# Closing the tile context ahead of the wait for the last stores in a Winograd convolution

## The chip, the core and the metric

The kernel runs on one core of one Trainium2 chip. The metric is the time of one execution on the device in microseconds (us); smaller is better. The core's engines run their own instruction streams and meet only through semaphores (counters): TensorE (PE in the profile, its weight loads PEld), VectorE (DVE), ScalarE (ACT), GpSimd (POOL) and SyncE (SP), which computes nothing and issues transfers. A name with a q behind it (SPq, POOLq) stands for that engine's sequencer.

## The reference

```python
def setup_inputs():
    batch, c_in, h, w, c_out = 16, 64, 64, 64, 128
    return {
        "x": np.random.randn(batch, c_in, h, w).astype(np.float32),
        "weight": np.random.randn(c_out, c_in, 3, 3).astype(np.float32) * 0.1,
    }

def reference(x, weight):
    x_pad = np.pad(x, ((0, 0), (0, 0), (1, 1), (1, 1)), mode='constant')
    output = np.zeros((batch, c_out, h, w), dtype=np.float32)
    ...
    output[b, co] += weight[co, ci, kh, kw] * x_pad[b, ci, kh:kh+h, kw:kw+w]
```

It is a 3x3 convolution with padding 1: 16 images of 64 channels and 64 x 64 points, 128 output channels. The input has 16.8 MB, the output 33.6 MB.

## The kernel before

**The work.** Two images are loaded as one pair, 128 partitions (two images times 64 channels) by 64 rows by 64 columns. There are 8 pairs, and each is worked off in 4 blocks of 8 row pairs. Over the rows the kernel uses a transformation that makes two output rows out of fewer products: GpSimd (for the first block VectorE) adds neighbouring rows to `ss`, ScalarE casts the rows to 16 bits in `xs`, TensorE multiplies in a loop of 8 rounds, one for each pair (L294 is the only matmul line of the loop), ScalarE copies two accumulators to `ut` (L204), and VectorE adds `ut` to the other accumulators and writes the output rows to a buffer called a home (L234).

**The transfers.** `load` is called by SyncE and by GpSimd; `store` (its transfer is on L109) by SyncE for the first image of a pair and by ScalarE for the second. The last pair's images go out in two pieces each, rows 0 to 32 and 32 to 64. A home that a later output uses again is guarded by a semaphore of its own (`s_out`). Every store whose home is used by nobody later counts on the one semaphore `s_end`, 16 for each store; `n_end` is the number of these stores.

**The order.** All of this stands in one critical section (L73, `tc.tile_critical`), in which the program itself sets every wait; each engine has its stream written out. When an engine has reached the end of the section it drains, and GpSimd waits for the drains of the others. Behind the section stand these two lines (L305 and L306):

```python
    tc.no_sync_barrier()
    SP.wait_ge(s_end, SP.to_reg(16 * n_end)).then_inc(s_done, 1)
```

The wait's threshold is moved to a register first. After it the function returns, the context `tc` is left (`with _tile.TileContext(nc) as tc:`, L332), and leaving it emits the closing instructions, which carry L332 in the profile: a few waits and a drain on SyncE; a crossing of all engines, in which each drains and reports and GpSimd gathers the reports and releases all; a drain and a clear of the context's semaphores on GpSimd (EVENT_SEMAPHORE_RANGE_CLEAR); and a second such crossing. The semaphores that are cleared there are those that were taken by `tc.alloc_semaphore`, through the helper `sem`, and a few of the context's own. L321 carries the instructions ahead of the program.

Of the kernel before, what the change touches and what calls it, by code (L numbers as in the profile page):

```python
# [25 lines left out]
def kernel(tc: tile.TileContext, x: bass.AP, weight: bass.AP, out: bass.AP):  # L26
    nc = tc.nc
# [3 lines left out]
    def sem(name):  # L31
        return tc.alloc_semaphore(name)
# [8 lines left out]
    s_act = sem("s_act")  # L41
    s_dve = sem("s_dve")
    s_out = {}
    s_end, s_done = sem("s_end"), sem("s_done")

    c_sum, c_cast, c_bank = sem("c_sum"), sem("c_cast"), sem("c_bank")

# [11 lines left out]
    PE, ACT, DVE, POOL, SP = nc.tensor, nc.scalar, nc.vector, nc.gpsimd, nc.sync  # L59
# [13 lines left out]
    with tc.tile_critical(sync_engine=EngineType.Pool):  # L73
# [51 lines left out]
        pieces, n_end = {}, 0  # L125
# [176 lines left out]
                                    mm.then_inc(s_pe, 1)  # L302
                            i += 1

    tc.no_sync_barrier()  # L305
    SP.wait_ge(s_end, SP.to_reg(16 * n_end)).then_inc(s_done, 1)  # L306


# [28 lines left out]
```

## Time and profile before

| | us |
|---|---|
| median of 3 runs | 126.46 |
| lowest and highest | 126.23, 126.65 |
| the profiled execution | 125.64 |
| its span, from the first to the last instruction of the program | 123.8 |

| engine | busy us | share of the span |
|---|---|---|
| TensorE (matmul) | 108.0 | 87% |
| VectorE | 84.1 | 68% |
| ScalarE | 67.2 | 54% |
| GpSimd | 38.9 | 31% |

The profile is of one execution. Its 1.84 us beside the span lie ahead of the first and behind the last instruction of the program and are not in the trace. Times inside the trace count from the first instruction. A row of the trace that names an engine, a line and an operation has its count, then minimum, median and maximum in ns, then the start of the first and of the last in us. A semaphore instruction's row shows when it fired and for how long it ran; the time that it waited before is in the list of waits. The page's slices cut the span in 40 equal parts of 3.1 us.

### The profile page before, as it was taken

The page shows a single profiled execution, that of the slowest core. Times are in us where ns is not written, and L with a number is a line of the kernel's source. Part 1 is how long each engine was busy: PE and PEld are TensorE (multiplying, and loading weights), DVE is VectorE, ACT ScalarE, POOL GpSimd, SP SyncE. Part 2 cuts the span into 40 slices and gives each one's busy share as a digit, 9 for nine tenths or more (in the row PEclk, how much of TensorE's full clock was granted, in tenths as well). Part 3 has the DMA queues.
Part 4 walks back from the last instruction along what each step waited for, and adds up shares of the span by engine and source line. Part 5 has one row for each costly group of instructions (what it writes and reads, how often), then busy time and mean ns, then how long its engine had stood idle before and what let it go on. Part 6 is the DMA issues. An engine that isn't in the chain of part 4 may idle for free.

```text
span 123.8 us, 2533 instructions
## 1 busy us (share of the span) xinstructions
PE 108.0 (87%) x989; PEld 56.7 (46%) x989; DVE 84.1 (68%) x133; ACT 67.2 (54%) x100; POOL 38.9 (31%) x30
## 2 busy tenths in 40 slices
PE   5969999999999999999999999999999999970000
PEld 1525555555555555555555555555555555530000
DVE  0067777877787778777877787788888887771000
ACT  4266656666666666666666566656665666520000
POOL 2207457170708270615054423233241103000000
PEclk9999999999999999999999999999999999999555
DMA  4999999999999999999999999999999999999993
GB/s 108 392 442 424 365 320 326 387 296 363 365 352 344 381 396 379 392 380 389 387 392 377 388 387 381 380 395 413 383 400 412 422 383 429 432 426 416 429 426 156
DMA packets 4467, 46.46 MB, mean 375 GB/s; under 512 B 496, under 2 KB 624, under 8 KB 1264
## 3 DMA queue, kind: packets, MB, share of 16 engines
q1 hardware_dynamic: 2160, 25.46, 50.0%
q10 hardware_dynamic: 1296, 16.78, 31.7%
q0 software_dynamic: 1008, 4.19, 16.6%
q14 instruction: 3, 0.02, 0.0%
HBM read 17.07 MB, written 33.55 MB: 409 GB/s over the span
## 4 chain that ended last, share of the span: by engine, by line
PE 82%; DVE 2%; DVEq 0%; issue 0%
PE bank L294 82%; DVE home L234 2%; DVEq L73 0%
## 5 line engine op out<-in xcount | busy, mean ns | idle before, releaser
L234 DVE TENSOR_TENSOR home<-bank,ut 128x512 f32<-128x512 f32 x128 | 81.9, 686 | 21.9 <-PE bank L294 21.7
L294 PE MATMUL bank<-xs,Wt 64*128 64x504 f16 (+3 forms) x768 | 87.5, 373 | 0.0
L294 PEld LDWEIGHTS bank<-xs,Wt 64*128 64x128 f16 x768 | 43.6, 94 | 38.6
L204 ACT COPY ut<-bank 128x512 f32<-128x512 f32 x64 | 34.4, 589 | 37.7 <-PE bank L294 37.7
L115 POOL TENSOR_TENSOR ss<-pair 128x1024 f16<-128x1024 f16 (+1 forms) x9 | 17.1, 1906 | 39.1 <-PE bank L294 32.4
L294 PE MATMUL bank<-ss,Wt 64*128 64x504 f16 (+1 forms) x192 | 26.5, 377 | 1.1 <-PEq L273 1.1
L115 POOL TENSOR_TENSOR ss<-home 128x1024 f16<-128x1024 f32 x7 | 16.5, 2364 | 14.5 <-PE bank L294 12.5
L121 ACT CAST xs<-home 128x1024 f16<-128x1024 f32 (+2 forms) x16 | 16.9, 1057 | 0.3 <-DMA home<-in_x_dram 0.3
L121 ACT COPY xs<-pair 128x1024 f16<-128x1024 f16 (+2 forms) x16 | 16.9, 1059 | 0.0
L294 PEld LDWEIGHTS bank<-ss,Wt 64*128 64x128 f16 x192 | 10.8, 94 | 10.8 <-issue 1.5
L95 POOL DMA_DIRECT2D pair<-in_x_dram x7 | 4.0, 577 | 8.6 <-DMA home<-in_x_dram 8.6
L248 PE MATMUL bank<-zeros 128*128 128x512 f16 x11 | 4.2, 540 | 1.4 <-DVE zeros L219 1.4
L220 DVE TENSOR_TENSOR Wt<-Wt 128x384 f16<-128x384 f16 x1 | 0.4, 358 | 4.8 <-ACT Wt L197 4.8
L197 ACT CAST Wt<-bank 128x384 f16<-128x384 f32 x3 | 1.2, 487 | 3.1 <-PE bank L257 3.1
L248 PEld LDWEIGHTS bank<-zeros 128*128 128x128 f16 x11 | 1.2, 124 | 3.1 <-DVE zeros L219 1.4
L197 ACT ACT_TABLE_LOAD x1 | 1.3, 1283 | 0.9 <-PEq L321 0.9
L257 PEld LDWEIGHTS bank<-ident,w 128*64 128x64 f16 x18 | 1.1, 209 | 1.0 <-POOL w L173 1.0
L173 POOL CAST w<-w_raw 128x576 f16<-128x576 f32 x1 | 0.7, 662 | 2.4 <-DMA w_raw<-in_weight_dram 2.4
L257 PE MATMUL bank<-ident,w 128*64 128x128 f16 x18 | 1.3, 299 | 0.1
L115 DVE TENSOR_TENSOR ss<-home 128x512 f16<-128x512 f32 x2 | 1.3, 688 | 0.0
L219 DVE MEMSET zeros<- 128x256 uint32 x1 | 0.3, 272 | 1.1 <-PEq L321 1.1
L221 DVE TENSOR_TENSOR Wt<-Wt 128x384 f16<-128x384 f16 x1 | 0.4, 359 | 0.0
(6 smaller groups left out, 0.9 us busy)
## 6 DMA issues: line engine op xcount, KB each, us to landing
out_dram<-home SPq DMA_DIRECT2D x7, 2048.0 KB, 23.0
out_dram<-home ACTq DMA_DIRECT2D x7, 2048.0 KB, 18.2
home<-in_x_dram SPq DMA_DIRECT2D x3, 2048.0 KB, 21.2
home<-in_x_dram SPq DMA_DIRECT2D x2, 1024.0 KB, 6.5
pair<-in_x_dram POOLq DMA_DIRECT2D x2, 1024.0 KB, 16.8
out_dram<-home SPq DMA_DIRECT2D x2, 1024.0 KB, 11.6
out_dram<-home ACTq DMA_DIRECT2D x2, 1024.0 KB, 11.1
pair<-in_x_dram POOLq DMA_DIRECT2D x3, 512.0 KB, 29.3
```

The source lines that it names most:

```text
L95: eng.dma_start(pairs[p][:, lo:hi, :], x_rows[128 * p : 128 * p + 128, lo:hi, :]).then_inc(s_in[p][k], 16)
L115: return eng.tensor_add(ss[:, lo : lo + n, :], v[:, lo : lo + n, 0, :], v[:, lo : lo + n, 1, :])
L121: return ACT.copy(xs[:, lo:hi, :], pairs[m // NB][:, lo:hi, :])
L173: when(POOL.tensor_copy(w16, w_raw), s_w, 16).then_inc(s_pool, 1)
L197: ACT.copy(wrow(g), flat[wp_bank[g]][:, 0 : 3 * CO]), s_pe, i + 1
L204: ACT.copy(uts[n % 2][b2], banks[(6 * n + b2) % 8]), s_pe, tiles(n, 1 + b2)
L220: when(DVE.tensor_sub(wrow(G21), wrow(G2), wrow(G1)), s_act, 2)
L221: when(DVE.tensor_sub(wrow(G01), wrow(G0), wrow(G1)), s_act, 3)
L234: DVE.tensor_add(rows(homes[OUT_HOME[p][b2]])[:, j0 : j0 + RB, i, :], banks[(6 * n + 2 + 2 * i + b2) % 8], uts[n % 2][b2],),
L248: PE.matmul(flat[7], zeros[:, 0:128], zeros)
L257: mm = PE.matmul(flat[wp_bank[g]][q : q + 64, k * CO : k * CO + CO], w16[:, t::9], ident)
L294: mm = PE.matmul(acc[b2][:, lo - j0 : hi - j0, c_lo:c_hi], Wt[p0 : p0 + 64, wi, kw, :], rhs, start=i == 0, stop=i == n - 1,)
```

## The change

The context is ended inside the function (`tc.close()`, which ends the trace of the body and goes to its end block) and compiled there (`tc.compile()`, which emits the closing instructions). SyncE's wait for the last stores is traced after that, with a constant instead of a register, and no longer increments `s_done`, which is gone. `s_end` is taken from `nc` instead of the context, so that the context's clear leaves it out; behind the wait SyncE clears it with an instruction of its own, and its number is given back, which emits nothing. When the `with` block is left, the context is compiled already.

```diff
     s_out = {}
-    s_end, s_done = sem("s_end"), sem("s_done")
+
+    s_end = nc.alloc_semaphore("s_end")
...
-    tc.no_sync_barrier()
-    SP.wait_ge(s_end, SP.to_reg(16 * n_end)).then_inc(s_done, 1)
+
+
+    tc.close()
+    tc.compile()
+    SP.wait_ge(s_end, 16 * n_end)
+    SP.sem_clear(s_end)
+    nc.release_semaphore(s_end)
```

## The prediction

> **What bounds the kernel now.** I read the page first, then the chain of work that ended last, then the end of the span piece by piece. The page's head, the two DMA lines of its slices and its HBM line:
>
> ```profile
> span 123.8 us, 2533 instructions
> ...
> DMA  4999999999999999999999999999999999999993
> GB/s 108 392 442 424 365 320 326 387 296 363 365 352 344 381 396 379 392 380 389 387 392 377 388 387 381 380 395 413 383 400 412 422 383 429 432 426 416 429 426 156
> ...
> HBM read 17.07 MB, written 33.55 MB: 409 GB/s over the span
> ```
>
> From the second slice to the last but one the 16 DMA engines are busy for 90% or more. So the transfers fill the span, and the last slice (3 tenths, 156 GB/s) is the only stretch at the end where they do not. The chain that ended last does not show this, because it is followed through engines and not through the stores:
>
> ```profile
> 7.92 101.44 PE bank L294 x948
> 109.36 1.90 DVE home L234 x3
> 111.26 0.60 DVEq L73
> ```
>
> It stops at 111.9 us, when the engines have nothing left to compute. What holds the remaining 11.9 us is seen in the timeline (start, duration) and in SyncE's own waits:
>
> ```profile
> 111.28 0.33 SPq L109 DMA_DIRECT2D out_dram<-home  x1
> 111.89 0.34 ACTq L109 DMA_DIRECT2D out_dram<-home  x1
> ```
>
> ```profile
> SPq L306 <- DMA out_dram<-home: 10.7, 1, 10.7
> SPq L332 <- PEq L332: 0.7, 2, 0.6
> ```
>
> L109 is the line of `store`: the last two stores are issued at 111.28 and 111.89. L306 is SyncE's wait for `s_end`, once, for 10.7 us. L332 is the line that opens the context: what its end emits carries that line. The stretches from there on, with DMA share and GB/s as the last two columns:
>
> ```profile
> core 0: us, PE busy (x) PEld busy (x) DVE busy (x) ACT busy (x) POOL busy (x), PEclk, DMA share, GB/s
> 111.90:112.90 1.00, 0.00 (x0) 0.00 (x0) 0.00 (x0) 0.00 (x0) 0.00 (x0) 1.00 0.82 344
> 112.90:114.00 1.10, 0.00 (x0) 0.00 (x0) 0.00 (x0) 0.00 (x0) 0.00 (x0) 1.00 1.00 425
> 114.00:116.00 2.00, 0.00 (x0) 0.00 (x0) 0.00 (x0) 0.00 (x0) 0.00 (x0) 0.58 1.00 426
> 116.00:118.00 2.00, 0.00 (x0) 0.00 (x0) 0.00 (x0) 0.00 (x0) 0.00 (x0) 0.50 1.03 434
> 118.00:120.00 2.00, 0.00 (x0) 0.00 (x0) 0.00 (x0) 0.00 (x0) 0.00 (x0) 0.50 0.98 418
> 120.00:122.00 2.00, 0.00 (x0) 0.00 (x0) 0.00 (x0) 0.00 (x0) 0.00 (x0) 0.50 0.92 389
> 122.00:122.30 0.30, 0.00 (x0) 0.00 (x0) 0.00 (x0) 0.00 (x0) 0.00 (x0) 0.50 0.01 0
> 122.30:123.80 1.50, 0.00 (x0) 0.00 (x0) 0.00 (x0) 0.00 (x0) 0.00 (x0) 0.50 0.00 0
> ```
>
> For ten microseconds only the stores run. They stop just after 122.0. Then come 1.5 us in which neither an engine nor a transfer does anything: this is where the change works.
>
> **The change part by part.** First the end as it stands, from the sequencer rows of lines 73 (the end of the critical section), 306 and 332 (count, min/median/max ns, first and last start):
>
> ```profile
> L73 SPq DRAIN  x1: 123/123/123, 111.7 to 111.7; - x1
> L73 ACTq DRAIN  x1: 153/153/153, 112.3 to 112.3; - x1
> L73 POOLq NOP  x1: 13/13/13, 112.5 to 112.5; - x1
> ```
>
> ```profile
> L306 SPq MOVE  x1: 40/40/40, 111.9 to 111.9; - x1
> L306 SPq EVENT_SEMAPHORE  x1: 17/17/17, 122.6 to 122.6; - x1
> ```
>
> ```profile
> L332 POOLq DRAIN  x1: 41/41/41, 112.5 to 112.5; - x1
> ...
> L332 SPq EVENT_SEMAPHORE  x1: 28/28/28, 122.7 to 122.7; - x1
> ...
> L332 SPq DRAIN  x2: 7/7/7, 122.9 to 122.9; - x2
> L332 POOLq EVENT_SEMAPHORE  x2: 17/17/17, 123.0 to 123.0; - x2
> ...
> L332 POOLq DRAIN  x1: 119/119/119, 123.1 to 123.1; - x1
> ...
> L332 PEldq EVENT_SEMAPHORE  x2: 51/51/51, 123.1 to 123.7; - x2
> ...
> L332 POOLq EVENT_SEMAPHORE  x2: 17/17/17, 123.6 to 123.7; - x2
> ...
> L332 POOLq EVENT_SEMAPHORE_RANGE_CLEAR  x1: 225/225/225, 123.3 to 123.3; - x1
> L332 SPq EVENT_SEMAPHORE  x1: 17/17/17, 123.7 to 123.7; - x1
> ```
>
> Read in order: SyncE's wait on `s_end` fires at 122.6. SyncE then passes its own context waits (122.7) and drains (122.9). GpSimd, already drained at 112.5, gathers the five engines and releases them (123.0), which the others see at 123.1. It drains again for 119 ns, clears the kernel's counters in 225 ns, gathers a second time and releases at 123.7. The last instruction is TensorE's receipt, 51 ns from 123.7. Nothing in this chain needs the stores. It stands behind them only because SyncE is the late one of the five.
>
> *Moved: the closing chain.* With the context closed ahead of SyncE's wait, the chain is started by whoever is last to leave the section: GpSimd's NOP at 112.5, as ScalarE drains at 112.3. It took 123.8 - 122.6 = 1.2 us, so it ends near 113.7. No DMA is in it, and it is moved past no issue: both last stores are issued by 112.2. Its cover is the stores in flight to 122.0 and the 10.7 us wait. Some 9 us of cover are left over. Without that cover, with the last store landing less than 1.2 us after its issue, it would cost the 1.2 us as now. As `s_end` stands among the ids to be cleared but is kept out, the clear may come as two; a second 225 ns lies under the same cover.
>
> *Removed:* the MOVE of 40 ns at 111.9, which went with the constant, and the increment of `s_done`. Both are worth nothing: the stores cover the first, and the wait's own 17 ns carry the second.
>
> *Added behind the wait:* one clear on SyncE. Behind it on SyncE nothing is queued, and nobody waits for it. It costs the pitch between two SyncE instructions, 0.1 us (122.6 to 122.7), and its own duration. No row shows a clear on SyncE. From below stands SyncE's 17 ns semaphore instruction; from above the same operation on GpSimd, 225 ns, for the counters of the whole kernel (29 are declared in it). One counter instead of those, and SyncE's drain at 7 ns where GpSimd's took 41 to 119, speak for less than 225. They do not say how much less. I take 0.1, halfway, and keep 0.02 and 0.225 for the range. The Trainium skill, page "Runtime: NRT & Kernel Launch", section "The ~15µs preamble/postamble breakdown", gives about 1.5 us for resetting 51 semaphores on an engine, an estimate of 0.03 us a counter. By it GpSimd's clear of 29 would have taken some 0.85 us; the row says 0.225, and the row decides. For SyncE's single counter 0.03 would make the forecast 0.07 us lower.
>
> *The sum.* The span now ends at 122.6 + 0.1 + 0.1 = 122.8 instead of 123.8: 1.0 us less. The profiled execution took 125.64 us, 1.84 more than its span; I leave that rest as it is, so it would come to 124.64. It lay 0.82 us under the median of the runs shown, 126.46. The tail taken off belongs to every execution, so I put the difference on the median: 126.46 - 1.0 = 125.46. Rounding of the rows (0.1), the price of the clear (0.08 below, 0.125 above) and the scatter of the runs (126.23 to 126.65, 0.2 to either side) make 125.1 to 125.8 of it. A difference of 0.3%, 0.38 us, is about what a measurement of this kernel can tell from none.
>
> **The rivals.** *The rest outside the span shrinks too.* Four engines would reach their end some 9 us early. What of the 1.84 us each of them must do after its last instruction would then lie under the stores. For it: the present chain ends on all five within one release. Against it: SyncE still has its own share to do, last. The largest crossing of all engines in the trace, SyncE's wait of 0.6 in its wait list, is what I give it: 125.46 - 0.6 = 124.86. The same page of the Trainium skill says that the closing barrier waits for all engines and that resets follow it; by that the rest stays at 1.84. No row here shows that part.
>
> *The second drain waits for the transfers.* The 119 ns drain on GpSimd has so far always run with all stores landed. If it held until they land, only the first crossing would be hidden. Then 122.6 is followed by drain, clear and release (123.1 to 123.7, 0.6) and SyncE's wait and clear (0.3): 123.5, a gain of 0.3, so 126.16. Against it: SyncE's drain at 111.7, ScalarE's at 112.3 and GpSimd's at 112.5 took 123, 153 and 41 ns with stores under way.
>
> *It doesn't do what it says.* If the closing chain were still emitted behind SyncE's wait, everything stays and a clear comes on top, 0.12 to 0.33 with its pitch: about 126.66. Against it stands only the order of the lines in the change.
>
> *Slower: the finished engines disturb the stores.* From 113.9 on four engines go on to whatever follows the program, resets of counters or queues, while 42 + 852 + 868 + 836 + 778 KB = 3.38 MB are still to be written (the rows from 113.9 to 122.0), in 8.1 us. At 344 GB/s, the lowest of those stretches, this would take 9.8 us: 1.7 us later, less the 1.0, so 127.16. It turns into a loss of over 0.3% below 3.38 / 9.5 = 356 GB/s. Against it: with all engines working, the nine slices up to 111 us kept 383 to 432 GB/s, so a few counter writes would have to weigh more than the whole kernel does.
>
> **How the numbers follow.** The forecast gets 0.76, the shrinking rest 0.12, the waiting drain 0.04, the unchanged order 0.04, the disturbed stores 0.04. Leaving out the last three, the range runs from the shrinking rest to the upper bound of the forecast with a tenth for its rounding: 124.8 to 125.9. Faster by over 0.3%: 0.75 + 0.12 = 0.87 (a hundredth of the forecast's chance lies above 126.08). Within 0.3%: 0.01 + 0.04 + 0.04 = 0.09. Slower: 0.04.
>
> **What would show it.** Right: GpSimd's range clear at 113 to 114 instead of 123.3; every engine but SyncE without an instruction after 114; SyncE with a wait of about 10 us for the stores, now behind its last barrier receipt; as the last instruction of the span a clear on SyncE, 0.1 to 0.3 us after the wait; a span of 122.7 to 122.95; the stores' rate from 114 to 120 still at 418 to 434 GB/s; execution time less span still 1.8. Wrong: the range clear still behind 122; the last store landing later than 122.6; a rest outside the span that has moved by more than 0.3; a clear on SyncE that takes over 0.3 us.

## The result and the profile after

The changed kernel takes 124.80 us (median of 4 runs, 124.64 to 125.32) against 126.46: a ratio of 0.988 (95% interval 0.9854 to 0.9906), faster by 1.66 us where 1.0 was forecast. Two more comparisons, made with the experiments below, gave 124.64 against 126.21 (0.987, 0.9824 to 0.9916) and 124.54 against 126.50 (0.9886, 0.9839 to 0.9933). Some kernels, the one before among them, now and then have an execution in a slower state, over 1.5% above their fastest, and all medians, spans and rests below that are taken over several executions leave these out.

The closing chain now carries L309, the line of `tc.compile()`, and the wait with the clear L311. The rows of L309 that answer to those of L332 before (count, min/median/max ns, first and last start):

```profile
L309 SPq EVENT_SEMAPHORE  x4: 17/22/440, 111.7 to 113.3; - x4
L309 POOLq DRAIN  x4: 40/60/95, 112.3 to 113.1; - x4
L309 POOLq EVENT_SEMAPHORE  x4: 17/17/17, 112.4 to 113.3; - x4
...
L309 PEldq EVENT_SEMAPHORE  x2: 51/51/51, 112.5 to 113.3; - x2
L309 POOLq EVENT_SEMAPHORE_RANGE_CLEAR  x2: 116/126/135, 112.7 to 113.0; - x2
```

```profile
L311 SPq EVENT_SEMAPHORE_RANGE_CLEAR  x1: 25/25/25, 123.6 to 123.6; - x1
```

SyncE's own waits:

```profile
SPq L311 <- DMA out_dram<-home: 10.3, 1, 10.3
SPq L309 <- PEq L309: 0.9, 2, 0.7
```

The whole chain lies between 111.7 and 113.4 (one drain of TensorE, which finished earlier, apart), two clears among it, and behind it SyncE waits 10.3 us for the stores. What follows the wait is one row: L310, the line of the wait, has none, so wait and clear became one instruction of 25 ns, and the span ends with it.

And yet the profiled span is only 0.2 us shorter, 123.6 for 123.8. Two rows show where the gain went in this execution: the time from issue to landing of ScalarE's last store, issued at 111.9 before and at 111.7 after. Before, then after:

```profile
DMA to landing us min/median/max: 10.7/10.7/10.7
```

```profile
DMA to landing us min/median/max: 11.9/11.9/11.9
```

In this execution the last store landed at 123.6, in that of before at 122.6. The stretches of the end (DMA share and GB/s last) show the stores thinning out for longer, rather than running slower throughout:

```profile
114.00:116.00 2.00, 0.00 (x0) 0.00 (x0) 0.00 (x0) 0.00 (x0) 0.00 (x0) 0.50 0.97 406
116.00:118.00 2.00, 0.00 (x0) 0.00 (x0) 0.00 (x0) 0.00 (x0) 0.00 (x0) 0.50 1.02 430
118.00:120.00 2.00, 0.00 (x0) 0.00 (x0) 0.00 (x0) 0.00 (x0) 0.00 (x0) 0.50 1.00 422
120.00:122.00 2.00, 0.00 (x0) 0.00 (x0) 0.00 (x0) 0.00 (x0) 0.00 (x0) 0.50 0.90 381
122.00:123.10 1.10, 0.00 (x0) 0.00 (x0) 0.00 (x0) 0.00 (x0) 0.00 (x0) 0.50 0.22 89
```

From 116 to 120 the rate is that of before; from 122 to 123.1 a fifth of the DMA engines' time is still used, where before nothing moved after 122.0. The old order can have such a tail too. A second profile of it, of the experiment close_alone below, has in the same stretch:

```profile
122.00:123.10 1.10, 0.00 (x0) 0.00 (x0) 0.00 (x0) 0.00 (x0) 0.00 (x0) 0.50 0.11 45
```

One more row in the page's list of queues is new:

```profile
q8 instruction: 1, 0.02, 0.0%
```

This is one packet of 16 KB of instructions. The list of queues for the stretch from 113.9 to 115.0 has it, among the last stores.

More of this execution's gain is outside the span. The profiled execution took 124.92 us, 1.3 more than its span, where before it was 1.8. The other three runs of the changed kernel have 125.32, 124.67 and 124.64 us with spans of 124.0, 123.4 and 123.3: 1.3 each time.

So two things had to be explained: why the rest outside the span fell by 0.5 us, and why the last store lands later in this profile. This table puts together what the profiled execution of every kernel said (us; rest is time less span; landing is counted from the issue of ScalarE's last store):

| kernel | its time | span | rest | landing | 16 KB packet |
|---|---|---|---|---|---|
| before | 125.64 | 123.8 | 1.8 | 10.7 | none |
| close_alone | 126.19 | 124.1 | 2.1 | 10.9 | none |
| changed | 124.92 | 123.6 | 1.3 | 11.9 | under the stores |
| changed, again | 124.72 | 123.4 | 1.3 | 11.6 | under the stores |
| changed, a third time | 124.51 | 123.1 | 1.4 | 11.3 | none |
| five_ahead | 124.92 | 123.6 | 1.3 | 11.7 | under the stores |
| five_behind | 126.66 | 124.4 | 2.3 | 10.8 | behind them |
| last_POOL | 125.97 | 123.0 | 3.0 | 11.2 | behind them |
| last_ACT | 126.51 | 124.2 | 2.3 | 12.4 | behind them |
| last_DVE | 124.84 | 123.4 | 1.4 | 11.7 | under the stores |
| last_PE | 125.34 | 123.8 | 1.5 | 11.9 | under the stores |
| hold_early | 124.84 | 123.5 | 1.3 | 11.7 | under the stores |
| hold_work | 124.28 | 122.9 | 1.4 | 11.0 | none |
| hold_mid | 124.93 | 123.6 | 1.3 | 11.5 | under the stores |

One execution of each kernel is not enough for this, as span and rest differ from one execution to the next. Time and span are on record for every execution of these kernels, but for the kernel before in the first comparison. The medians of these are (us):

| kernel | executions | span, median | rest, median | rest, lowest to highest |
|---|---|---|---|---|
| before, last three comparisons | 54 | 124.3 | 1.98 | 1.73 to 2.97 |
| close_alone | 9 | 124.1 | 2.03 | 1.73 to 2.81 |
| changed, three comparisons | 16 | 123.05 | 1.48 | 1.27 to 2.45 |
| five_ahead | 4 | 123.7 | 1.36 | 1.32 to 1.41 |
| five_behind | 10 | 124.7 | 2.05 | 1.99 to 2.27 |
| last_POOL | 9 | 123.1 | 2.52 | 1.79 to 2.97 |
| last_ACT | 5 | 123.4 | 1.48 | 1.45 to 2.31 |
| last_DVE | 9 | 123.1 | 1.62 | 1.38 to 2.51 |
| last_PE | 3 | 123.0 | 1.89 | 1.54 to 2.00 |
| hold_early | 12 | 123.5 | 1.42 | 1.26 to 2.41 |
| hold_work | 6 | 123.0 | 1.50 | 1.26 to 2.31 |
| hold_mid | 5 | 123.5 | 1.49 | 1.30 to 1.88 |

The median span fell by 1.25 us and the median rest by 0.5. So the 0.2 us above compare a short execution of the kernel before (8 of the 54 have 123.8 or less) with a long one of the changed kernel (2 of the 16 have 123.6 or more). Nor is it shown that the change makes the last store land later. With 1.1 us between landing and end in the old order and next to nothing in the new one, as in the profiles, the medians put the landing at 123.2 before and 123.0 after, an estimate.

### The profile page after: what moved, and what is told of

It reads as the page before. It is cut to its first block, busy times and chain, and to the rows that moved or that the text cites. A ratio compares the mean times of both kernels' runs of the same rounds, so it can differ in the third digit from the quotient of the medians.

```text
span 123.6 us, 2534 instructions
## 1 busy us (share of the span) xinstructions
PE 108.0 (87%) x989; PEld 57.1 (46%) x989; DVE 84.1 (68%) x133; ACT 67.2 (54%) x100; POOL 38.9 (31%) x30
## 4 chain that ended last, share of the span: by engine, by line
PE 82%; DVE 2%; DVEq 0%; issue 0%
PE bank L295 82%; DVE home L235 2%; DVEq L74 0%
## 5 line engine op out<-in xcount | busy, mean ns | idle before, releaser
L295 PEld LDWEIGHTS bank<-ss,Wt 64*128 64x128 f16 x192 | 10.9, 94 | 10.6 <-issue 1.4
```

What stands on the lines that cost most here:

```text
L295: mm = PE.matmul(acc[b2][:, lo - j0 : hi - j0, c_lo:c_hi], Wt[p0 : p0 + 64, wi, kw, :], rhs, start=i == 0, stop=i == n - 1,)
```

## The experiments

**The wait on each of the other engines.** One edit, four times:

```diff
-    SP.wait_ge(s_end, 16 * n_end)
-    SP.sem_clear(s_end)
+    POOL.wait_ge(s_end, 16 * n_end)     # then ACT, DVE, PE
+    POOL.sem_clear(s_end)
```

> The wait for the last stores and its clear stand on GpSimd in place of SyncE; all else as in the changed kernel. In the changed kernel the rest outside the span is 1.3 us where it was 1.84, and a packet of 16 KB of instructions that lay outside the span before now runs at 114.0 under the stores. Theory A: one engine fetches code after its part of the program; it was 0.5 us of the rest. If that engine is GpSimd, this packet moves behind the stores, the rest returns to about 1.8 us and the time to about 125.4; if not, the rest stays at 1.3 us and the time near 124.9. Theory B: the rest shrank because a crossing of all engines shortens when four of them are early, whoever is last: rest 1.3 us. Theory C: SyncE has the shortest way out: rest 1.8 us on every other engine. GpSimd's clear of 0.12 us in place of SyncE's 0.025 is in addition in the span.

> The same with the wait and the clear on ScalarE. A: rest 1.8 us and time 125.4 if ScalarE is the engine that fetches, else 1.3 us and 124.8. B: 1.3 us. C: 1.8 us.

> The same with the wait and the clear on VectorE. A: rest 1.8 us and time 125.4 if VectorE is the engine that fetches, else 1.3 us and 124.8. B: 1.3 us. C: 1.8 us.

> The same with the wait and the clear on TensorE. A: rest 1.8 us and time 125.4 if TensorE is the engine that fetches, else 1.3 us and 124.8. B: 1.3 us. C: 1.8 us. Over the four runs A expects 1.8 us on one or two engines, B on none, C on all.

Measured against 126.47 us of the kernel before: 125.39 us on GpSimd (0.9919, 0.9885 to 0.9953), 124.89 on ScalarE (0.9894, 0.9845 to 0.9943), 124.84 on VectorE (0.9903, 0.9868 to 0.9939), 124.89 on TensorE (0.9889, 0.9825 to 0.9952). The median rests are 2.5, 1.5, 1.6 and 1.9 us, where the kernel before has 1.9 in this comparison and the changed kernel 1.5. B, which wanted 1.3 on all, falls on GpSimd; C, which wanted 1.8 on all, falls on ScalarE and VectorE; TensorE's three executions decide nothing. Of A it holds that in the profiles the packet moved behind the stores on GpSimd and on ScalarE. But GpSimd's rest grew past the 1.8 us that A foresaw, and a packet that belongs to one engine's code should have moved for one. GpSimd is the slowest place for the wait, by 0.5 us over the medians of the other three, though the intervals of all four overlap. ScalarE's profiled execution, 126.51 us, was the slowest of its five (the others took 124.85 to 124.98 with rests of 1.45 to 1.49), so its rest of 2.3 and its landing are those of an unusual one. The clear took, on GpSimd:

```profile
L311 POOLq EVENT_SEMAPHORE_RANGE_CLEAR  x1: 44/44/44, 122.9 to 122.9; - x1
```

**The close alone, behind the wait.**

```diff
     SP.wait_ge(s_end, SP.to_reg(16 * n_end)).then_inc(s_done, 1)
+    tc.close()
+    tc.compile()
```

> The order of the kernel before with one part of the change alone: the context is closed and compiled inside the function, but behind SyncE's wait, which keeps its register and s_done. Theory A (the gain is the place of the closing chain) expects no change: 126.5 us, chain of 1.1 us behind the wait, 1.84 us outside the span. A rival in which the explicit close or compile emits something shorter expects some of the 1.66 us gained.

126.36 us against 126.21: 1.0005 (0.9974 to 1.0036). No change, as A said. Its chain stands behind the wait as before, from the wait's firing to TensorE's last receipt:

```profile
L306 SPq EVENT_SEMAPHORE  x1: 17/17/17, 123.0 to 123.0; - x1
```

```profile
L308 PEldq EVENT_SEMAPHORE  x2: 51/51/51, 123.5 to 124.1; - x2
```

This is a second profile of the old order: 1.1 us of chain, and a rest of 2.1 us. The small parts of the change, the constant for the register, the missing increment and `s_end` outside the context, were not run alone; of the first, the MOVE ran at 111.9, under the stores.

**More crossings, ahead of the wait and behind it.** The changed kernel with five crossings of all engines:

```diff
     tc.compile()
+    for _ in range(5):
+        nc.all_engine_barrier()     # five_ahead
     SP.wait_ge(s_end, 16 * n_end)
     SP.sem_clear(s_end)
     nc.release_semaphore(s_end)
+    for _ in range(5):
+        nc.all_engine_barrier()     # five_behind
```

> The changed kernel with five more crossings of all engines between the closing chain and SyncE's wait. One crossing is about 0.3 us in the trace (SyncE's drain at 112.33 to its next at 112.62), so five are 1.5 us. If the stores cover whatever stands ahead of the wait, the time stays at 124.8 us and the rest outside the span at 1.3 us. If sequencer work under the stores delays them, up to 1.5 us more.

> The changed kernel with the same five crossings behind SyncE's wait and clear. They are then on the path: 1.5 us more in the span. Theory A2, that the rest outside the span fell from 1.84 to 1.3 us because four engines reached their end early, expects the rest back at 1.84 us, as all five now end together: 124.8 + 1.5 + 0.5 = 126.8 us. Theory B2, that the rest fell for another reason (another place of the code, a fetch), expects 1.3 us and 126.3 us.

Ahead of the wait the time is 125.06 us (0.9898, 0.9843 to 0.9953), 0.4 above the changed kernel's 124.64 in the same comparison, with its runs (124.92 to 125.11) inside the scatter of that (124.37 to 125.11). Behind it the time is 126.71 us, and the gain is gone (1.0035, 0.9997 to 1.0073). The crossings' rows, ahead and then behind:

```profile
L311 SPq DRAIN  x5: 7/7/7, 113.6 to 114.9; - x5
...
L311 PEldq EVENT_SEMAPHORE  x5: 51/51/51, 113.8 to 115.3; - x5
```

```profile
L314 SPq DRAIN  x5: 7/7/7, 122.8 to 124.1; - x5
...
L314 PEldq EVENT_SEMAPHORE  x5: 51/51/51, 122.9 to 124.3; - x5
```

The same instructions run for about 1.7 us in both places (113.6 to 115.3; from SyncE's clear at 122.7 to the end at 124.4). Under the stores this costs 0.4 us, which the intervals do not tell from nothing; behind them it costs 2.1 us (126.71 against 124.64), of which 1.7 are the crossings. The median rest outside the span is 2.05 us behind and 1.36 ahead, where the changed kernel itself has 1.48. So A2 is borne out: when all five engines come to their end together, the way out of the program is longer than when four are long gone. The size fits as well. A2 named 126.8 us and B2 126.3, and the ten runs lie between 126.50 and 127.57.

**The changed kernel again.**

> The changed kernel itself beside the others on one chip, for a second profile and a narrower interval: 124.8 us, ratio 0.987, rest outside the span 1.3 us; the last store's landing differs from run to run by some tenths of a us, the wait and clear behind it take under 0.05 us.

The median is 124.64 us. Against close_alone of the same comparison the two profiled executions differ by 126.19 - 124.72 = 1.47 us. This adds up from 1.1 (the chain behind the wait), 0.7 to 0.8 (rest 2.1 to 1.3), less 0.4 (the last landing, 123.0 to 123.4). Over the executions of this comparison, span and rest have medians of 124.2 and 1.96 us before and of 122.95 and 1.52 after, so that the span gives 1.25 and the rest 0.44.

**Where the packet goes.** All landings so far lay at 10.7 to 11.2 us when the packet was not among the stores and at 11.6 to 11.9 when it was, ScalarE's unusual execution apart. So theory P says that the packet holds up the stores of one DMA engine, and theory Q that the landings scatter by themselves. These three kernels hold ScalarE back, so as to move the packet behind the stores. Each gives one store a semaphore of its own for it, ScalarE's last but one in hold_early and hold_work, SyncE's last in hold_mid:

```diff
+        lo, hi, _ = pieces[NP - 1, 1, 1]          # hold_mid: [NP - 1, 0, 3]
+        pieces[NP - 1, 1, 1] = (lo, hi, s_mid)
+        n_end -= 1
...
     tc.compile()
+    ACT.wait_ge(s_mid, 16)
+    ACT.sem_clear(s_mid)
+    for k in range(5):                            # hold_work alone
+        hold = ACT.copy(xs[:, 8 * k : 8 * k + 8, :], banks[0])
+    hold.then_inc(s_ack, 1)                       # hold_work alone
+    ACT.wait_ge(s_ack, 1)                         # hold_work alone
+    ACT.sem_clear(s_ack)                          # hold_work alone
     SP.wait_ge(s_end, 16 * n_end)
```

> The changed kernel, in which ScalarE is held back behind the closing chain until its last store but one has landed (about 118.5 us; this store counts on a semaphore of its own). So far every kernel whose 16 KB packet of instructions ran under the stores had its last landing 11.6 to 11.9 us after the last issue, every one whose packet ran behind them 10.7 to 11.2 us, but for one run of 12.4. Theory P: the packet holds up the stores of one DMA engine by about its 0.93 us. It then still runs under the stores, near 120: landing 11.6 to 11.9 us after the issue, rest 1.3 us, time 124.7. Theory Q: the landings scatter by themselves. Same time.

> As hold_early, and ScalarE then makes five copies of 128x512 into a buffer that nobody reads (0.6 us each), so that it ends about 1 us before the last landing. With the wait on ScalarE itself the packet started 1.4 us after ScalarE's end and the rest was 2.3 us; so the packet would start about 0.4 us behind the last landing and ScalarE's way out would end with SyncE's. P: landing 10.7 to 11.2 us after the last issue, rest 1.3 to 1.5 us, time 124.0. Q: no change, 124.7 us.

> As hold_work, but ScalarE waits for SyncE's last store, which lands about 0.6 us before the last of all, and makes no copies. P: the packet runs well behind the stores, landing 10.7 to 11.2 us after the last issue, but ScalarE's way out of 2.3 us from there sets the end: rest 1.7 us, time 124.3. Q: rest 1.7 us with landings as they are now, 125.0 us.

> The changed kernel beside these three on one chip: 124.7 us, landing 11.6 to 11.9 us after the last issue, rest 1.3 us, under both theories.

Medians against 126.50: hold_early 124.96 (0.9884, 0.9849 to 0.992), hold_work 124.79 (0.9899, 0.985 to 0.9947), hold_mid 124.93 (0.9887, 0.9837 to 0.9937), the changed kernel 124.54 (0.9886, 0.9839 to 0.9933). None beats the changed kernel, and the 124.0 and 124.3 us that P wanted of hold_work and hold_mid did not come. The premise fell with hold_early and hold_mid: ScalarE ended at 119.3 and 123.0, and the packet still ran between 114.0 and 115.8 in both.

```profile
L314 ACTq EVENT_SEMAPHORE_RANGE_CLEAR  x1: 46/46/46, 123.0 to 123.0; - x1
```

So it does not wait for ScalarE's end, and the third profile of the changed kernel shows that it need not come at all: its list of queues ends with the line for q14 and has none for q8. What remains is a comparison, not a control. Seven profiled executions with the packet among the stores have landings of 11.5 to 11.9 us; six without it there have 10.7 to 11.3, and one, the unusual one of last_ACT, 12.4. Within the changed kernel it is 11.9 and 11.6 with the packet and 11.3 without, at 124.92, 124.72 and 124.51 us. That fits P, at 0.3 to 0.6 us of landing within the changed kernel. In time less is at stake: of that kernel's 16 executions the six with a span of 123.3 or more have a median of 124.80 us, the other ten 124.54. For Q speaks that the spans of the kernel before, 123.7 to 125.6, scatter more widely than those of the changed one, 122.7 to 124.0. Since no kernel moved the packet at will, P is not shown, and Q is not excluded. What issues the packet stays open as well, and so does when it comes in the old order: neither of its profiles has it, so that it lay outside the span there, as the first expectation has it, is not shown.

## Why the prediction was right, and where its size was off

The chain went under the stores as forecast, and the time, 124.80, sits on the lower end of the range, 124.8 to 125.9. The forecast's own bounds, 125.1 to 125.8, do not reach it; the range does, as it took in the first rival. By the prediction's own steps:

- *The cover.* The chain was to end near 113.7 with some 9 us of cover left. It ends at 113.4, and 10.3 us of waiting follow. five_ahead put 1.7 us more under the same cover for 0.4 us, no clear cost.
- *The clear as two.* It came as two, of 116 and 135 ns in place of one of 225, both hidden.
- *The term of the added clear was mis-sized.* It stood at 0.1 for the pitch and 0.1 for the clear. The pitch does not exist, as the wait became part of the clear, and SyncE's clear takes 25 ns, at the low end of the bounds (0.02 to 0.225). The chain's 1.2 us of the sum, 1.1 when rounding is taken out, is gained whole instead of 1.0. The median spans, 1.25 us shorter, bear this out.
- *The rest outside the span was left at 1.84.* This was the step that cost most. It fell to 1.3 in all four runs of the first comparison, and its median by 0.44 and 0.47 in the two others. The first rival, with a chance of 0.12, had named this and put it at 0.6. Its sum of 124.86 is close to what was measured, partly by luck: the 0.6 was borrowed from a wait inside the trace. The forecast's 125.46 is 0.66 too high, about 0.15 for the clear and 0.5 for the rest. The argument against the rival, that SyncE still has its own share to do, is true (1.3 us remain at the least) but says nothing of the others' shares, which now lie under the stores; with GpSimd last the median rest is 2.5 us. The Trainium skill, page "Runtime: NRT & Kernel Launch", section "The ~15µs preamble/postamble breakdown", has a closing barrier that waits for all engines. That the rest would therefore stay at 1.84 is what the prediction made of it, and it does not hold for this kernel: with SyncE last the median rest is 1.5 us, with all five together 2.0.
- *The waiting drain* did not occur: GpSimd's drains of 40 to 95 ns passed between 112.3 and 113.1 with stores in flight. *The unchanged order* did not occur either.
- *The disturbed stores* did not occur as priced: the rate was 422 to 430 GB/s from 116 to 120, not 344 throughout. In the changed kernel's three profiles the last landing came 0.4 to 1.2 us later after its issue than in the two of the old order. But the median span is shorter by the whole 1.1 us of the tail, so a loss by late landings is not shown.
- *Of the signs to look for*, the range clear (112.7 and 113.0), the four engines' silence after 114 and the 10 us wait behind the last receipt came. The profiled span, 123.6, is not within 122.7 to 122.95, as the landing was late; of the 16 executions four are. A clear 0.1 to 0.3 us behind the wait did not come, and the rate from 114 to 116, 406 GB/s, was under the 418 named. Two signs listed under wrong did come: the last store landed later than 122.6, and the rest moved by 0.5, more than 0.3.

The sum was put on the median, 126.46, although the profiled execution of before lay 0.82 under it. The old order's second profile, 0.17 under its own median, has a rest of 2.1 in place of 1.8: the rest varies, 1.73 to 2.97 over the 54 executions, and the first profile was at its short end.

## What to carry to other kernels

Look at what runs between the last transfer's landing and the end of the program, and ask of each step whether it needs that transfer; a closing chain that only needs the engines can run under the last stores. The engine that waits last should be the one with the least to do afterwards, and the others should be let go early: what they do behind the program counts too, though no row shows it. A span that barely moves from one profile to another does not refute such a change: compare the landing, the tail behind it and the time outside the span one by one, and take span and rest over all executions before explaining what one of them shows.

## What the hardware showed that was not expected

A wait followed by a clear of the same counter on one engine ran as one instruction, 25 ns on SyncE, 44 on GpSimd, 46 on ScalarE. A crossing of all five engines costs 0.34 us (five in 1.7 us). The time outside the span depends on who ends last and how early the others are gone: its median is 1.5 us with SyncE or ScalarE last, 1.6 with VectorE, 2.5 with GpSimd, and 2.0 when all end together. Single executions overlap (1.27 to 2.45 for SyncE, 1.79 to 2.97 for GpSimd). And a packet of 16 KB of instructions can run among a program's last stores once most engines have finished, in some executions of the same kernel and not in others.
